# Attention's row maxima, transposed and sent in two halves by query

## The chip, the cores and the metric

The kernel runs on one core of one Trainium2 chip. The metric is device time in microseconds of one execution, lower is better. Engines are named as in the profile: PE (TensorE matmul) with PEld (its weight loads), DVE (VectorE), ACT (ScalarE), POOL (GpSimd), SP (SyncE, whose queue issues nearly all DMAs).

## The reference, cut to what matters

Two transformer layers over 1024 tokens of width 1024, in fp32. Layer 0 mixes with forgetting attention ("fox", 12 heads of 64), layer 1 with latent attention ("mla", 12 heads of 96 with rotary parts). Each layer has 4 more heads that attend to 256 memory tokens, then an output projection and a convolutional feed-forward part. The part around the change is the softmax:

```python
def causal_block_attention(q, k, v, log_decay=None):
    ...
        logits = jnp.einsum('bhqd,bhkd->bhqk', qc, k).astype(jnp.float32)
        if log_decay is not None:
            logits = logits + args[2][..., None] - log_decay[:, :, None, :]
        ...
        logits = jnp.where(key_idx[None, :] <= q_idx[:, None], logits, -jnp.inf)
        p = jax.nn.softmax(logits, axis=-1).astype(v.dtype)
        return jnp.einsum('bhqk,bhkd->bhqd', p, v)

def memory_cross(qm, k_mem, v_mem, q_gain, k_gain):
    ...
    logits = jnp.einsum('bshd,bmhd->bhsm', q, k).astype(jnp.float32)
    p = jax.nn.softmax(logits, axis=-1).astype(v_mem.dtype)
    return jnp.einsum('bhsm,bmhd->bshd', p, v_mem).reshape(b, s, MEM_WIDTH)
```

## The kernel before, in words

Scores are computed transposed, with keys on the partitions and queries along the free axis, so that the exponentials can be multiplied with V at once. A query's maximum must then be known before its scores are computed: it enters the score product as one more row. `QA` holds a head's queries (64 or 96 rows, plus rows for the decay), and its row `h.mrow` (66 or 96) holds minus the maximum of each of the 1024 queries; `KA` holds ones in that row. A causal head's score products read `QA[0:67]` or `QA[0:97]`. Operands are split into a high and a low part for accuracy; the passes with `KB` or `QB` add the low parts and don't read the row of maxima.

`maxpass(h)` (lines 290 to 315) finds the maxima. It computes a head's scores once with queries on the partitions, in chunks: 10 for a causal head (`CAUSAL_MAX`, lines 59 to 70; the first three cover query tiles 0 to 3, the others tiles 4 to 7), 4 for a memory head (`FULL_MAX`, line 71, two query tiles each). A chunk takes a PSUM buffer `psX` (one of 3, shared with the transposes of queries and keys and with projections), and DVE reduces it: `tensor_reduce` without a mask (L299) or `tensor_tensor_reduce` with the causal mask (L304). The maxima land in `mA`, 128 x 8. `final` (lines 308 to 313) transposes `mA` on PE into a `psX` (8 x 128), DVE negates it into `mrow` (L312), and SP sends it in one DMA into the row of `QA` (L313).

The main loop (lines 428 to 471) goes over 16 heads. A head is cut into units: six groups of two key tiles in a causal head (`CAUSAL_GROUPS`), two in a memory head (`FULL_GROUPS`), and for each group one unit that adds low-part products of an earlier group (`lo`), two units of scores, two of products with V (`hi`): 30 and 10 units in all. Groups 0 and 1 of a causal head are queries 0 to 511, groups 2 to 5 queries 512 to 1023; a memory head's group 0 and group 1 are the two halves. So a head's first scores are its unit 2, and those of the second half begin at unit 12 (causal) or 7 (memory).

Between the units stand the side pieces of later heads: the next head's maxima chunks and `final`, preparation (`prep`: transposes and splits of K and Q) of the next head (`leads` 1) or the one after (`leads` 2), and background work (`bg`: layer 1's group projections). A piece has a position between 0 and 1, and it is run when the count of units done exceeds the position times the units of the head (line 458). Positions stand in `TIMES` (lines 279 to 284), one entry per layer: `max2` and `final2` for causal heads with `leads` 2, `max1`, `final1` with `leads` 1, `max_mem` and `final_mem` while a memory head runs.

Layer 0 runs 12 fox heads, then 4 memory heads, all with `leads` 2. Layer 1 runs 4 memory heads, then 12 mla heads, the first five heads with `leads` 2, the others 1. In layer 1 PE's instructions are kept in program order (`pin[0] = not offset`, line 409); in layer 0 a scheduler orders all engines by priority and by its own model of when operands are ready. Every engine and the SP queue run their instructions in the order in which they stand. `norm1` and `norm2` (lines 392 to 406) divide by the sums on DVE (L404) and send rows over SP (L395 to L399).

```python
add(chunks, *times["max2" if h.causal else "max_mem"])
side.append((times["final2" if h.causal else "final_mem"], final))
...
while side and side[0][0] * total < done:
    side.pop(0)[1]()
```

Of the kernel before, what the change touches and what calls it, by code (L numbers as in the profile page):

```python
# [12 lines left out]
OP = mybir.AluOpType  # L13
# [61 lines left out]
def hybrid_kernel(ctx: ExitStack, tc: tile.TileContext, A, out):  # L75
# [197 lines left out]
    def slot(name="slot", dt=F32):  # L273
# [3 lines left out]


    TIMES = [
        {"prep2": ((0.15, 0.97), (0.25, 0.97)), "max2": (0.0, 0.68), "final2": 0.68, "max_mem": (0.24, 0.75),  # L280
         "final_mem": 0.7, "norm": (7, 24, 27)},
        {"prep1": (0.0, 0.23), "max1": (0.28, 0.76), "final1": 0.8, "prep2": ((0.55, 1.0), (0.38, 1.0)),
         "max2": (0.0, 0.72), "final2": 0.63, "max_mem": (0.0, 0.63), "final_mem": 0.82, "norm": (7, 20, 23)},
    ]

    def attention(L, heads, leads, offset=0, bg=None, fill={}):
# [3 lines left out]
        def maxpass(h):  # L290
            mA = small.tile([P, 8], F32, name="mA")

            def chunk(segs):
                px = psX()
                for qt, k0, nk, off, own, on in segs:
                    mm(px[:, off:off + nk], h.max_q(qt), h.max_k(k0, nk), True, True)
                if not segs[0][4]:
                    q0, n, width = segs[0][0], len(segs), segs[0][2]
                    nc.vector.tensor_reduce(mA[:, q0:q0 + n],  # L299
                                            px[:, :n * width].rearrange("p (a b) -> p a b", a=n), axis=AX, op=OP.max)  # L300
                    return
                for qt, k0, nk, off, own, on in segs:
                    m = mA[:, qt:qt + 1]
                    nc.vector.tensor_tensor_reduce(px[:, off:off + nk], px[:, off:off + nk], mQ[:, 512 - nk:],  # L304
                                                   scale=1.0, scalar=m if on else NEG, op0=OP.add, op1=OP.max,
                                                   accum_out=m)

            def final():
                px = psX()
                transpose(px[:8, :P], mA[:, 0:8], ident)  # L310
                row = small.tile([8, P], F32R, name="mrow")
                nc.vector.tensor_scalar(row, px[:8, :P], -1.0, None, op0=OP.mult)  # L312
                nc.sync.dma_start(h.QA[h.mrow:h.mrow + 1, :].bitcast(F32), row.bitcast(F32))  # L313

            return [lambda c=c: chunk(c) for c in h.max_chunks] + [final]

        def score_units(h, g):
            half, parts = h.groups[g]
# [91 lines left out]
        n = len(heads)  # L410
        later, pend, los = [], [], []
        with tc.high_priority(offset=offset):
            pieces = heads[0].prep() + maxpass(heads[0]) + (heads[1].prep() if leads[1] == 2 else [])
            for i, f in enumerate(pieces):
                f()
                for u in fill.get(i, ()):
                    u()
# [7 lines left out]
                    a[1]()  # L425

        pl.mark = []
        for i, h in enumerate(heads):
            pl.mark.append(tc.cur_priority)
            side = []  # L430

            def add(pieces, a, b):
                side.extend((a + (b - a) * j / len(pieces), f) for j, f in enumerate(pieces))

            if i + 1 < n:
                if leads[i + 1] == 2:
                    *chunks, final = rest if i else maxpass(heads[1])
                    add(chunks, *times["max2" if h.causal else "max_mem"])
                    side.append((times["final2" if h.causal else "final_mem"], final))
                else:  # L440
                    add(heads[i + 1].prep(), *times["prep1"])
                    *chunks, final = maxpass(heads[i + 1])
                    add(chunks, *times["max1"])
                    side.append((times["final1"], final))
            if i + 2 < n and leads[i + 2] == 2:
                add(heads[i + 2].prep(), *times["prep2"][heads[i + 2].row % 2])
                rest = maxpass(heads[i + 2])
# [1333 lines left out]
```

## Time and profile before

| | us |
|---|---|
| median of 3 runs | 2527.43 (2526.28 to 2527.52) |
| the profiled execution, its own time | 2524.9 |
| its span, first to last instruction | 2523.2 |
| PE busy | 2366.4 |
| DVE busy | 1890.5 |
| ACT busy | 1209.2 |
| POOL busy | 980.0 |

The profile is one execution. Busy is the time in which an engine runs at least one instruction; PE's matmuls are pipelined, their ends are modelled, and starts are what can be compared. A wait is idle time of an engine before an instruction, put down to what ended it. PEclk is the granted clock of PE as a share of 2.4 GHz; it is either 1.0 or 0.5 at a time, and a mean over a stretch says how much of it ran at which.

### The profile page before, as it was taken

Reading aid. Unit: us, or ns where it says so; the run is one execution under the profiler, and the core shown is the slowest. Engines: PE = TensorE matmul, PEld = TensorE weight load, DVE = VectorE, ACT = ScalarE, POOL = GpSimd, SP = SyncE. Lnnn points to the kernel's source line nnn. Section 1 sums busy time; section 2 is a strip of 40 time slices with the busy share of each in tenths; the row PEclk is TensorE's granted clock in tenths of the full one; section 3 lists DMA queues with packets and bytes.
Section 4 is the critical chain, followed back from the end, with each engine's and each line's share of the span. In section 5 each row is a group of like instructions: output and inputs, shape, how many; then the busy total and the mean of one; then the engine's idle time right before and its main releaser. Section 6 shows DMA issues by size and latency. Waiting matters only on the chain.

```text
span 2523.2 us, 32480 instructions
## 1 busy us (share of the span) xinstructions
PE 2366.4 (94%) x11609; PEld 1952.9 (77%) x11609; DVE 1890.5 (75%) x3183; ACT 1209.2 (48%) x2341; POOL 980.0 (39%) x640
## 2 busy tenths in 40 slices
PE   7999899998999999989998798879979999998999
PEld 7999666677788888868888676657868888886887
DVE  7432787747778878799997878774488788778997
ACT  5544677723444444434454555555244444443443
POOL 1221467743233233234322566666142333233342
PEclk9999899999999999999999799989999999998999
DMA  4221122252132232541230101010512222225221
GB/s 143 84 51 27 35 61 48 52 182 104 51 92 76 84 92 76 196 154 50 102 134 10 35 22 29 19 38 17 193 60 84 90 77 84 84 84 233 92 101 67
DMA packets 163651, 208.89 MB, mean 83 GB/s; under 512 B 11175, under 2 KB 124682, under 8 KB 163490
## 3 DMA queue, kind: packets, MB, share of 16 engines
q1 hardware_dynamic: 162054, 206.63, 25.8%
q8 instruction: 92, 1.51, 0.2%
q14 instruction: 69, 0.57, 0.1%
q10 hardware_dynamic: 1436, 0.18, 0.0%
HBM read 153.34 MB, written 39.98 MB: 77 GB/s over the span
## 4 chain that ended last, share of the span: by engine, by line
PE 74%; DVE 18%; issue 3%; DMA 3%; ACT 2%; POOL 1%; SPq 0%; DVEq 0%; ACTq 0%; POOLq 0%
PE psX L102 32%; PE psS L102 24%; PE psO L102 15%; DVE f_op L90 2%; PE psX L106 2%; DVE f_x L1156 1%; DVE mA L299 1%; DVE psX L304 1%; DVE f_S L90 1%; POOL f_op L90 1%; DVE KB L525 1%; DVE QB L525 1%; DVE f_d L90 1%; PE psS L106 1%; DVE f_T L90 1%
## 5 line engine op out<-in xcount | busy, mean ns | idle before, releaser
L90 POOL TENSOR_TENSOR f_op<-f_S,f_op 128x512 fp32r<-128x512 f32 x184 | 271.0, 1475 | 670.0 <-ACT f_op L83 613.1
L102 PE MATMUL psS<-f_T,f_op 128*128 128x512 f32 x1584 | 382.2, 393 | 7.8 <-DVE f_T L90 5.9
L90 POOL TENSOR_TENSOR plo<-pf,ph 128x1024 fp32r<-128x1024 f32 (+2 forms) x160 | 312.7, 1966 | 155.0 <-ACT pf L343 96.0
L102 PEld LDWEIGHTS psS<-f_T,f_op 128*128 128x128 f32 x1584 | 297.1, 189 | 68.9 <-DVE f_T L90 6.5
L102 PE MATMUL psX<-f_B,f_op 128*128 128x512 f32 x1260 | 296.3, 389 | 0.1
L83 ACT CAST f_op<-f_S 128x512 fp32r<-128x512 f32 x248 | 153.6, 621 | 269.6 <-PE psS L102 103.2
L102 PEld LDWEIGHTS psX<-f_B,f_op 128*128 128x128 f32 x1260 | 236.4, 188 | 49.6 <-issue 0.5
L102 PE MATMUL psS<-f_op 128*128 128x512 f32 x960 | 222.4, 390 | 1.6 <-DVE f_op L90 1.5
L102 PEld LDWEIGHTS psS<-f_op 128*128 128x128 f32 x960 | 180.6, 188 | 40.1 <-DVE f_op L90 2.4
L102 PE MATMUL psX<-f_op 128*128 128x512 f32 x666 | 174.5, 403 | 19.9 <-DVE f_op L90 16.5
L102 PE MATMUL psX<-w_w,hTh 128*128 128x384 f32 (+2 forms) x672 | 168.1, 334 | 2.2 <-ACT hTh L83 2.2
L102 PEld LDWEIGHTS psX<-f_op 128*128 128x128 f32 x666 | 128.1, 194 | 52.4 <-DVE f_op L90 21.7
L83 ACT CAST f_op<-f_raw 128x512 fp32r<-128x512 f32 x148 | 91.4, 622 | 136.2 <-PE psS L102 70.4
L342 ACT ACTIVATE ph<-psS 128x1024 fp32r<-128x1024 f32 (+2 forms) x131 | 112.3, 858 | 87.7 <-PE psS L102 79.1
L898 DVE SCALAR_TENSOR_TENSOR f_v<-f_cv,cw,f_v 128x1023 f32<-128x1023 f32 x88 | 150.2, 1706 | 5.0 <-ACT f_v L896 3.5
L102 PE MATMUL psX<-KA,QA 66*128 66x128 f32 (+4 forms) x320 | 110.3, 392 | 28.9 <-DVE mA L299 11.3
L83 ACT CAST f_op<-f_d 128x512 fp32r<-128x512 f32 x144 | 84.3, 619 | 102.0 <-PE psS L102 35.6
L858 DVE TENSOR_TENSOR f_u<-psS,f_p 128x512 f32<-128x512 f32 x44 | 30.4, 691 | 126.6 <-PE psS L102 126.6
L102 PEld LDWEIGHTS psX<-w_w,hTh 128*128 128x128 f32 x672 | 120.9, 190 | 3.2 <-ACT hTh L83 2.8
L898 DVE SCALAR_TENSOR_TENSOR f_v<-f_cg,cw,f_v 128x1023 f32<-128x1023 f32 x88 | 112.7, 1280 | 11.0 <-ACT f_v L896 11.0
L90 POOL TENSOR_TENSOR f_op<-f_d,f_op 128x512 fp32r<-128x512 f32 x52 | 74.1, 1425 | 116.9 <-ACT f_op L83 112.8
L102 PE MATMUL psS<-QA,KA 67*128 67x512 f32 (+7 forms) x304 | 110.0, 363 | 8.3 <-DMA QA<-mrow 8.3
(379 smaller groups left out, 5693.2 us busy)
## 6 DMA issues: line engine op xcount, KB each, us to landing
f_raw<-in_ffn_w_up_dram SPq DMA_DIRECT2D x88, 512.0 KB
g<-f_v SPq DMA_DIRECT2D x44, 512.0 KB
f_d<-g SPq DMA_DIRECT2D x36, 512.0 KB
f_d<-in_ffn_w_down_dram SPq DMA_DIRECT2D x36, 512.0 KB
w_raw<-in_fox_w_in_dram SPq DMA_DIRECT2D x48, 192.0 KB
rrow<-rec SPq DMA_DIRECT2D x32, 256.0 KB
wo_raw<-in_w_out_dram SPq DMA_DIRECT2D x32, 256.0 KB
xr<-x SPq DMA_DIRECT2D x16, 512.0 KB
```

The lines of the kernel that those rows point to most:

```text
L83: nc.scalar.copy(o, i)
L90: return (nc.vector if eng == "v" else nc.gpsimd).tensor_tensor(o, a, b, op=OP.subtract)
L102: r = nc.tensor.matmul(*a, **k)
L106: r = nc.tensor.transpose(*a, **k)
L299: nc.vector.tensor_reduce(mA[:, q0:q0 + n], px[:, :n * width].rearrange("p (a b) -> p a b", a=n), axis=AX, op=OP.max)
L304: nc.vector.tensor_tensor_reduce(px[:, off:off + nk], px[:, off:off + nk], mQ[:, 512 - nk:], scale=1.0, scalar=m if on else NEG, op0=OP.ad ...
L342: nc.scalar.activation(ph, ps[:, :w], AF.Exp)
L525: nc.vector.scalar_tensor_tensor(Tl[tl0:tl1, hs], px, gcol, Th[0:n, hs].bitcast(F32), op0=OP.mult, op1=OP.subtract)
L858: nc.vector.tensor_tensor(o, x, y, op=OP.add)
L898: nc.vector.scalar_tensor_tensor(v[:, k:], src[:, :S - k], cw[:, 2 - k, ch:ch + 1], v[:, k:], op0=OP.mult, op1=OP.add)
L1156: nc.vector.tensor_tensor(X[t][:, hs], X[t][:, hs], self.sets[st][v], op=OP.add)
```

## The change

The transposition of `mA` is cut in two, by query halves. `final(half)` transposes 4 columns, negates 4 x 128 and sends 512 values into its half of the row. The first half is placed one and a half chunk intervals behind the chunk after which all its maxima are known (`first`, 3 for causal heads, 2 for memory heads), so behind the chunk with index 4 of 10 or 3 of 4. The second half is carried over into the head itself, to position 0.08: after unit 3 of a causal head and after unit 1 of a memory head. The chunks' stretches in `TIMES` end later (0.68 to 0.85 in layer 0's `max2`, 0.76 to 0.92 in layer 1's `max1`, and so on); the `final` positions go. The first head of a layer runs both halves one after the other, where it ran `final` before.

```diff
     TIMES = [
-        {"prep2": ((0.15, 0.97), (0.25, 0.97)), "max2": (0.0, 0.68), "final2": 0.68, "max_mem": (0.24, 0.75),
-         "final_mem": 0.7, "norm": (7, 24, 27)},
-        {"prep1": (0.0, 0.23), "max1": (0.28, 0.76), "final1": 0.8, "prep2": ((0.55, 1.0), (0.38, 1.0)),
-         "max2": (0.0, 0.72), "final2": 0.63, "max_mem": (0.0, 0.63), "final_mem": 0.82, "norm": (7, 20, 23)},
+        {"prep2": ((0.15, 0.97), (0.25, 0.97)), "max2": (0.0, 0.85), "max_mem": (0.24, 0.85), "norm": (7, 24, 27)},
+        {"prep1": (0.0, 0.23), "max1": (0.28, 0.92), "prep2": ((0.55, 1.0), (0.38, 1.0)),
+         "max2": (0.0, 0.85), "max_mem": (0.0, 0.8), "norm": (7, 20, 23)},
     ]
...
-            def final():
+            def final(half):
                 px = psX()
-                transpose(px[:8, :P], mA[:, 0:8], ident)
-                row = small.tile([8, P], F32R, name="mrow")
-                nc.vector.tensor_scalar(row, px[:8, :P], -1.0, None, op0=OP.mult)
-                nc.sync.dma_start(h.QA[h.mrow:h.mrow + 1, :].bitcast(F32), row.bitcast(F32))
-
-            return [lambda c=c: chunk(c) for c in h.max_chunks] + [final]
+                transpose(px[:4, :P], mA[:, half * 4:half * 4 + 4], ident)
+                row = small.tile([4, P], F32R, name="mrow")
+                nc.vector.tensor_scalar(row, px[:4, :P], -1.0, None, op0=OP.mult)
+                nc.sync.dma_start(h.QA[h.mrow:h.mrow + 1, half * 512:half * 512 + 512].bitcast(F32), row.bitcast(F32))
+
+            first = max(j for j, segs in enumerate(h.max_chunks) if segs[0][0] < 4) + 1
+            return [lambda c=c: chunk(c) for c in h.max_chunks], first, [lambda i=i: final(i) for i in range(2)]
...
+            chunks, first, ends = maxpass(heads[0])
+            pieces = heads[0].prep() + chunks + [lambda: [f() for f in ends]] + (heads[1].prep() if leads[1] == 2 else [])
...
+        carried = []
         for i, h in enumerate(heads):
-            side = []
+            side, carried = carried, []
...
-                    *chunks, final = rest if i else maxpass(heads[1])
-                    add(chunks, *times["max2" if h.causal else "max_mem"])
-                    side.append((times["final2" if h.causal else "final_mem"], final))
+                    chunks, first, ends = rest if i else maxpass(heads[1])
+                    span = times["max2" if h.causal else "max_mem"]
                 else:
                     add(heads[i + 1].prep(), *times["prep1"])
-                    *chunks, final = maxpass(heads[i + 1])
-                    add(chunks, *times["max1"])
-                    side.append((times["final1"], final))
+                    chunks, first, ends = maxpass(heads[i + 1])
+                    span = times["max1"]
+                add(chunks, *span)
+                side.append((span[0] + (span[1] - span[0]) * (first + 1.5) / len(chunks), ends[0]))
+                carried.append((0.08, ends[1]))
```

## Rows read from the trace of the kernel before

**Rows 1.** The page: engine, busy us, share of the span, instructions.

```profile
PE 2366.4 (94%) x11609; PEld 1952.9 (77%) x11609; DVE 1890.5 (75%) x3183; ACT 1209.2 (48%) x2341; POOL 980.0 (39%) x640
```

**Rows 2.** Waits of PE, 277 to 515 us: us in total, times, longest.

```profile
PE psX L106 <- DVE mA L304: 9.2, 9, 2.2
PE psS L102 <- DMA QA<-mrow: 3.6, 2, 2.2
PE psX L102 <- DVE mrow L312: 2.7, 1, 2.7
```

**Rows 3.** Waits of PE, 1360 to 1765 us.

```profile
PE psX L102 <- DVE mA L299: 11.3, 8, 5.0
...
PE psX L106 <- POOL gk L93: 7.9, 4, 4.2
PE psX L106 <- DVE mA L304: 7.7, 4, 2.7
PE psS L102 <- DMA QA<-mrow: 4.7, 3, 3.3
PE psX L106 <- DVE mrow L312: 3.0, 1, 3.0
```

**Rows 4.** Windows: length, busy us (count) of PE, PEld, DVE, ACT, POOL; PEclk, DMA share, GB/s.

```profile
291.00:475.00 184.00, 169.44 (x939) 123.11 (x938) 148.60 (x309) 143.88 (x214) 128.75 (x69) 0.95 0.22 51
...
1450.00:1740.00 290.00, 253.15 (x1508) 196.33 (x1508) 216.83 (x454) 163.37 (x251) 187.25 (x118) 0.95 0.10 27
```

**Rows 5.** PE groups: count | busy, mean ns | idle before; whole span, then 283:520.

```profile
L106 PE MATMUL psX<-ident,mA 128*8 128x128 f32 x32 | 9.5, 297 | 13.9 <-DVE mA L304 11.5 <-DVE rs_y L233 1.4 <-DVE mA L299 1.1
...
L106 PE MATMUL psX<-ident,mA 128*8 128x128 f32 x15 | 4.2, 282 | 3.8 <-DVE mA L304 3.8
```

**Rows 6.** PE in order of time, layer 1: start, us, instruction [idle before].

```profile
1574.95 0.27 PE L106 MATMUL psX<-ident,mA 128*8 128x128 f32 x1 [1.68 <-DVE mA L304]
...
1579.19 0.64 PE L106 MATMUL psX<-ident,gk 128*96 128x128 f32 x4 [1.26 <-POOL gk L93]
...
1600.42 0.39 PE L102 MATMUL psO<-ph,g_vh 128*65 128x512 f32 x1
1600.65 0.40 PE L102 MATMUL psO<-ph,g_vl 128*64 128x512 f32 x1
1600.97 0.27 PE L106 MATMUL psX<-ident,mA 128*8 128x128 f32 x1
1601.00 0.45 PE L102 MATMUL psX<-g_w,LTh 128*128 128x192 f32 x2
```

**Rows 7.** DVE in order of time, the same boundary of two heads in layer 1.

```profile
1574.09 0.75 DVE L304 CUSTOM_DVE_ANT_0 psX<-psX,mQ,mA 128x512 f32<-128x512 f32 x1
...
1577.57 0.27 DVE L312 TENSOR_SCALAR mrow<-psX 8x128 fp32r<-8x128 f32 x1
...
1577.97 1.71 DVE L93 TENSOR_TENSOR gk<-gk,rs_y 128x512 f32<-128x512 f32 x2
```

**Rows 8.** SP's issues of the row, and the scores that waited for it.

```profile
473.81 0.69 SPq L313 DMA_DIRECT2D QA<-mrow  x1
...
477.68 0.50 PE L102 MATMUL psS<-QA,KA 67*128 67x512 f32 x1 [1.40 <-DMA QA<-mrow]
...
1473.58 0.70 SPq L313 DMA_DIRECT2D QA<-mrow  x1
...
1475.43 0.79 PE L102 MATMUL psS<-QA,KA 97*128 97x512 f32 x1 [3.33 <-DMA QA<-mrow]
```

**Rows 9.** PE, layer 0: last score of group 0 with the row, first of group 2, two heads.

```profile
342.97 0.34 PE L102 MATMUL psS<-QA,KA 67*128 67x384 f32 x1
...
345.69 0.40 PE L102 MATMUL psS<-QA,KA 67*128 67x512 f32 x1
...
426.04 0.34 PE L102 MATMUL psS<-QA,KA 67*128 67x384 f32 x1
...
430.64 0.40 PE L102 MATMUL psS<-QA,KA 67*128 67x512 f32 x1
```

More of the change, by code (lines that the diff above doesn't have):

```diff
@@ L412, in attention @@
         with tc.high_priority(offset=offset):
-            pieces = heads[0].prep() + maxpass(heads[0]) + (heads[1].prep() if leads[1] == 2 else [])
+            chunks, first, ends = maxpass(heads[0])
+            pieces = heads[0].prep() + chunks + [lambda: [f() for f in ends]] + (heads[1].prep() if leads[1] == 2 else [])
             for i, f in enumerate(pieces):
```

## The prediction

> **What bounds the kernel now.** I read the page's engine shares first, then TensorE's waits in the two attention stages, then windows, then the time lines around the places that the change moves. TensorE is busy 94% of the span and VectorE 75% [rows 1], so the time goes where TensorE's idle time goes. The change touches only attention: about 283 to 520 us (layer 0) and 1370 to 1760 us (layer 1). Its possible gain is what TensorE loses there, not a share of the whole.
>
> What it loses is written in two tables. In layer 0 it waited 9.2 us at transposes until VectorE had finished masked maxima (L304), 3.6 us in front of scores until the row of maxima had landed, 2.7 us for a PSUM buffer that the row's negation (L312) still held [rows 2]. In layer 1: 11.3 us for unmasked maxima (L299), 7.7 for masked ones, 4.7 for the row; and 7.9 for keys that GpSimd scales, which this change doesn't touch [rows 3]. The windows add the clock: in 184 us of layer 0 and in 290 us of layer 1 the mean grant was 0.95 of full speed [rows 4]. The two levels are 2.4 and 1.2 GHz, so a tenth of these stretches, 18 and 29 us, ran at 1.2 GHz; at the higher level that work takes half as long, so 9 + 14.5 = 23.5 us are lost in this way.
>
> **The change, part by part.** Its positions are counted in units of a head (30 in a causal head, 10 in a memory head). Layer 0, causal: the last maxima moves from unit 19 to 23, the transpose of the first half from 21 to 12; the second half's goes to unit 3 of the head itself. Layer 1, causal: last maxima 22 to 26, first half 25 to 18, second half again unit 3. A head's first scores are its unit 2, those that need the second half its unit 12 (memory heads: transposed at 1, needed at 7).
>
> *1. The transpose no longer stands behind its own maxima.* All transposes of maxima waited 13.9 us, 1.4 of it (for rs_y) in the first head, which the change leaves as it is; layer 0's share is 3.8 [rows 5], so layer 1's is 8.7. The first half now follows its last maxima by two and a half intervals, the second by 7 to 10 units. Layer 0's 3.8 us and 3.7 us around layer 1's memory heads go whole. The other 5.0 us are three waits of 1.68 us, one of them in the rows, each followed 4 us later by a wait for scaled keys of about 1.3 us [rows 6]: TensorE arriving earlier would wait longer there, unless VectorE, which gets to the keys only after the maxima and the negation [rows 7], is earlier too. I count half, 2.5. Together -10.0, with bounds -7.5 and -12.5.
>
> *2. The first scores no longer wait for the row.* 8.3 us in both layers [rows 2, 3]. The first half leaves 7 to 9 units earlier between causal heads. Between memory heads of layer 0 it leaves at unit 8 of 10 as now, so the 2.2 us there stays. I take -5.0, bounds -3 and -6.1.
>
> *3. Maxima spread wider.* Their interval grows from 2.04 to 2.55 units in layer 0 and from 1.44 to 1.92 in layer 1. They share three psX buffers with transposes and projections; the waits that this can shorten are layer 1's 11.3 us for L299 maxima, 5.4 us of layer 0's 9.2, and the 2.7 and 3.0 for L312 [rows 2, 3, 5], some 22 us. But nothing in VectorE's work shrinks, and maxima now run into the stretch in which the next head's operands are split. I take a little under a quarter, -5.0; bounds +5 (they collide there) and -12.
>
> *4. Clock.* 23.5 us are lost to the lower level [rows 4]; idle time in these windows is 14.6 + 36.9 = 51 us, of which parts 1 to 3 take 20, or two fifths. Proportionally that gives back 9; spells at 1.2 GHz also follow waits that stay, so I take -4.0; bounds 0 and -9.
>
> *5. One more transpose for each of 32 heads.* Around one that waited for nothing, TensorE started 0.32 us after a 512-column matmul that itself had started 0.23 after the one before, and the next instruction came 0.03 later [rows 6]: about 0.09 + 0.03 = 0.12 us more than without it. A half has four columns where a whole has eight; the trace has no such transpose, so between 0 and the 0.30 us mean of a record [rows 5] I take 0.1: +3.2 (0 to +9.5).
>
> *6. The second half's row must come in time.* The trace of before has no such wait. The way from the transpose is 0.27 us, as long for the negation [rows 6, 7], 0.1 between them and to the issue, and then the landing: a whole row issued at 1473.58 let the scores go at 1475.43, 1.85 us later, and one at 473.81 only at 477.68, 3.87 us later [rows 8]. **Does half a row land sooner?** The trace has only whole rows, and I price the half like the whole, 1.85, with 0.9 as the low end (in proportion to bytes) and 3.9 as the high. The Trainium skill (DMA: Bandwidth & Descriptors, section Anatomy of one DMA) says the setup and completion part, about 2.0 us for the path it fits, depends on nothing of the transfer, which speaks against splitting: by it two halves cost two landings and part 6 stays at +6, by proportion it would be near 0. No run here shows it yet. So 2.5 us are needed plus VectorE's queue, which is in order: the negation can stand behind other work, 2.35 us of it in the case of [rows 6, 7]. The cover is 8 units. In layer 0, score to score, it was 2.72 us in one head and 4.60 in another [rows 9]; in layer 1, where 290 us hold some eleven heads [rows 4], eight of 30 units are 7 us. So layer 0's 11 causal heads are exposed by about 0.3 us on average (0 to 1.5), and seven memory heads, with 5 units, by 0.4: +6 (0 to +21).
>
> *7. VectorE, SP and POOL.* 32 more negations of 0.27 us [rows 7] are 9 us on an engine that is busy 81% of one window and 75% of the other [rows 4]; a quarter shows: +2 (0 to +9). SP issues 32 more transfers of about 0.7 us [rows 8]; behind a late row on that queue stand the copies QA to QB and KA to KB of the head after next, needed most of a head later, so I count 0. POOL gets nothing.
>
> **Sum.** -10.0 - 5.0 - 5.0 - 4.0 + 3.2 + 6 + 2 = -12.8 us. Against the profiled execution's own 2524.9 us: 2512.1. The median of the runs stands 2.5 us above that execution, so I predict 2514.6 us.
>
> **Rivals.** *A. The waits only move.* Keys that GpSimd scales (7.9 us, [rows 3]) and VectorE's queue set the end of layer 1's pairs, and layer 0's gain is eaten by part 6. For it: the two waits of [rows 6], one behind the other. Against it: VectorE has a quarter of its time free. Then parts 1 to 4 give only 11 against 11 of cost: 2527, within 2523 to 2532. 18%.
>
> *B. A bigger gain.* The late row is what holds each second head of layer 0, and without it waits and clock come back at the bounds: -12.5 - 6.1 - 8 - 7 against 7 of cost (part 6 at 2) make -27 us, 2500. 18%.
>
> *C. Slower: the second half's row is late in each head.* In layer 0 the negation stands behind VectorE's products with the reciprocals or psX maxima, and TensorE stops at unit 12. At 1.5 us for 11 heads and 1.0 for 7, part 6 is 23.5; 4 us of clock given back turn into 4 lost, so the sum is -20 + 5.2 + 23.5 + 4 = +12.7: 2540. It decides from a mean of about 1.0 us over the 18 heads, where the gains of parts 1 to 4 (24, less 5.2 of other cost) are used up. Against it: layer 0's instructions aren't pinned to program order (line 409), and other matmuls can fill. 10%.
>
> *D. The split isn't one.* If the second write to the row held up all readers of that buffer, the scores of units 7 and 8 would wait for it, some 1.5 us in 27 causal and memory heads with the clock behind it: some 2550 (the forecast without part 6, and 40 us). 4%.
>
> **How the numbers follow.** The forecast has 50%, from 2506 to 2522. About 5 us, 0.2%, is what a measurement of this kernel can tell from no change. Faster by more: forecast and B, 0.68; within: A, 0.18; slower: C and D, 0.14. The range 2498 to 2534 reaches over A, most of B and a third of C; left out are B's far end, most of C, and D, some 16%.
>
> **What would show it.** Right: transposes of maxima wait under 2 us in all outside the first head; scores' waits for the row under 5 us; grants in both windows 0.96 or more; 64 transposes and 64 negations. Wrong: a score of 67 or 97 rows in a head's third group with a wait of over 1 us for the row in most heads (C), in the second group (D); waits for scaled keys grown by what the transposes lost (A). I would be wrong altogether if TensorE's idle time in both stages stayed while the waits changed names.

## The result and the profile after

The changed kernel takes 2544.24 us (median of 4 runs, 2539.81 to 2544.85), the kernel before 2526.86 us beside it: a ratio of 1.0076, 95% interval 1.0060 to 1.0091. It is **slower** by 15 to 23 us, 0.8%; 2514.6 us had been forecast, and the measurement lies beyond the range. The profiled execution after took 2543.93 us with a span of 2542.2.

Page of the changed kernel, engine shares, to set beside [rows 1]:

```profile
PE 2376.0 (93%) x11641; PEld 1960.3 (77%) x11641; DVE 1905.8 (75%) x3215; ACT 1210.3 (48%) x2341; POOL 976.7 (38%) x640
```

TensorE and VectorE each have the 32 instructions more that the change adds, and busy times 9.6 and 15.3 us longer. TensorE's waits in layer 0 (277 to 525 us: us in total, times, longest), to set beside [rows 2]; the wait in the last line is the only one of its kind in the whole span:

```profile
PE psO L102 <- DVE oh L85: 7.2, 2, 5.8
PE psX L102 <- DVE mA L303: 4.0, 2, 2.5
...
PE psX L106 <- DVE mA L303: 2.6, 2, 1.7
...
PE psS L102 <- DMA QA<-mrow: 0.2, 1, 0.2
```

The same view of layer 1 (1360 to 1765 us), beside [rows 3]; L298 and L303 are the unmasked and masked maxima that were L299 and L304:

```profile
PE psX L102 <- DVE mA L298: 20.8, 13, 5.5
PE psX L106 <- DVE gq L93: 8.5, 4, 2.7
PE psX L106 <- DVE mA L303: 7.5, 4, 3.6
PE psX L106 <- DVE mA L298: 7.0, 2, 4.4
...
PE psX L106 <- DVE gk L93: 2.9, 3, 1.0
```

What the change was to remove is gone: scores waited 8.3 us for a row before [rows 2, 3] and 0.2 us in the whole span after. What it was to relieve grew. Layer 1's wait for unmasked maxima in front of chunks and projections, 11.3 us in [rows 3], is 20.8 us, with 7.0 at transposes (2.2 before), and the wait for keys that GpSimd scales (7.9 us, with 0.9 for queries on VectorE) is replaced by 8.5 + 2.9 us for queries and keys that VectorE scales. Transposes of maxima, which should no longer wait, waited as long as in [rows 5]. Their group in the changed kernel (count, min/median/max ns, first and last start; then idle time by what ended it):

```profile
L106 PE MATMUL psX<-ident,mA x64: 269/273/421, 281.1 to 1755.8; 128*4 128x128 f32 x64
...
  DVE mA L303: 8.5, 5
  DVE mA L298: 3.5, 2
```

With 2.0 us for three other operands that is 14.0 us against 13.9, though not at the same places: the three waits of 1.7 us in layer 1's pairs of heads are gone, and waits of 2.61 us (at 1438.86), 3.65 (1477.54), 1.56 (1719.74) and 0.74 stand at other boundaries. The windows, beside [rows 4], show that the clock went the other way too:

```profile
291.00:475.00 184.00, 166.71 (x909) 119.20 (x908) 150.53 (x307) 137.79 (x205) 123.72 (x67) 0.94 0.21 48
1450.00:1740.00 290.00, 248.05 (x1458) 194.56 (x1457) 221.72 (x465) 162.03 (x247) 175.80 (x118) 0.92 0.10 28
```

A mean grant of 0.92 between the levels 2.4 and 1.2 GHz is 16% of 290 us, 46 us, at 1.2 GHz where it was 29; half of the additional 17 us is lost time. TensorE gets through 1458 matmuls in a window that held 1508, though the windows hold work a few us apart, since layer 1 starts 8.5 us later.

Over the whole of each stage, layer 0 and layer 1, the kernel before and then the changed one (length, busy us of PE to POOL, PEclk, DMA share, GB/s):

```profile
282.20:620.00 337.80, 311.76 (x1575) 233.03 (x1575) 241.76 (x487) 201.93 (x299) 193.44 (x105) 0.95 0.30 83
1386.90:1762.50 375.60, 325.84 (x1863) 252.53 (x1862) 271.12 (x555) 206.84 (x316) 231.85 (x147) 0.92 0.10 26
```

```profile
281.10:628.00 346.90, 315.81 (x1591) 233.74 (x1591) 251.78 (x502) 200.19 (x296) 192.99 (x104) 0.94 0.28 80
1395.40:1781.00 385.60, 330.14 (x1872) 258.60 (x1871) 277.23 (x571) 208.08 (x316) 224.92 (x147) 0.90 0.10 26
```

Layer 0 is 9.1 us longer and layer 1 10.0. TensorE's idle time, length less busy, grew by 5.1 and 5.7 us; the rest is busy time, 4.1 and 4.3 us more, for a few more transposes and at lower grants.

**Where in layer 1.** One boundary of two heads, the pattern of [rows 6, 7]. TensorE, then VectorE, in order of time:

```profile
1593.70 0.61 PE L106 MATMUL psX<-ident,gk 128*96 128x128 f32 x4 [0.96 <-DVE gk L93]
...
1597.78 1.09 PE L106 MATMUL psX<-ident,gq 128*96 128x128 f32 x4 [2.68 <-DVE gq L93]
```

```profile
1592.21 0.75 DVE L303 CUSTOM_DVE_ANT_0 psX<-psX,mQ,mA 128x512 f32<-128x512 f32 x1
...
1592.88 3.18 DVE L93 TENSOR_TENSOR gk<-gk,rs_y 128x512 f32<-128x512 f32 x2
1595.98 2.61 DVE L93 TENSOR_TENSOR gq<-gq,rs_y 128x768 f32<-128x768 f32 x2
```

In the kernel before, behind the gk of [rows 7]:

```profile
1579.61 3.04 DVE L93 TENSOR_TENSOR gq<-gq,rs_y 128x768 f32<-128x768 f32 x2
```

The late maxima stand ahead of the next head's keys and queries in VectorE's queue. TensorE takes its instructions in program order here, so the transposes of gk and gq hold it, and behind them the scores. The two scalings of gk took 3.18 us where [rows 7] had 1.71; those of gq took 2.61 where they had 3.04. From one transpose of maxima to the one a pair of heads later (1559.46 to 1614.24 here, 1574.95 to 1628.35 before) TensorE waits 7.2 us in place of 6.0, and the pair takes 54.8 us in place of 53.4. The pairs are not all of layer 1's loss: from its first transpose of maxima to the fifth head's row of sums (issued at 1487.43 before, 1500.61 after) it takes 4.7 of its 10 us more, and there waits for unmasked maxima of 4.39, 3.09 and 2.61 us stand between the memory heads.

**Where in layer 0.** The boundary whose scores [rows 9] show at 342.97 and 345.69. TensorE, then VectorE:

```profile
341.74 0.50 PE L102 MATMUL psX<-KA,QA 66*128 66x128 f32 x2 [1.52 <-DVE mA L303]
343.21 0.27 PE L106 MATMUL psX<-ident,mA 128*4 128x128 f32 x1 [0.97 <-DVE vh L1382]
...
347.12 0.40 PE L102 MATMUL psS<-QA,KA 67*128 67x512 f32 x1
```

```profile
338.57 2.48 DVE L530 SCALAR_TENSOR_TENSOR KB<-k,g_cols,KA 64x512 fp32r<-64x512 f32 x1
...
342.27 0.74 DVE L303 CUSTOM_DVE_ANT_0 psX<-psX,mQ,mA 128x512 f32<-128x512 f32 x1
```

L530 splits operands of the head after next. The last maximum ends at 343.01, behind such splits, and the second half's transpose starts at 343.21. Its first score starts at 347.12, 1.43 us later than in the kernel before, but no wait stands in front of that one: TensorE had other work. At the end of the layer a single wait of 5.81 us stands before the products with V: the copy of their PSUM buffer stood in VectorE's queue behind two products that took 5.64 us. VectorE there, and GpSimd:

```profile
517.59 5.64 DVE L93 TENSOR_TENSOR oh<-oh,rrow 128x512 f32<-128x512 f32 x2 [1.20 <-DMA rrow<-rec]
523.15 0.68 DVE L85 COPY oh<-psO 65x512 f32<-65x512 f32 x1
```

```profile
517.58 5.10 POOL L90 TENSOR_TENSOR plo<-pf,ph 128x1024 fp32r<-128x1024 f32 x2 [3.15 <-ACT pf L344]
```

### The profile page after: what moved, and what is told of

Same layout as the page of the kernel before. It is cut to its first block, busy times and chain, and to the rows that moved or that the text cites. A ratio compares the mean times of both kernels' runs of the same rounds, so it can differ in the third digit from the quotient of the medians.

```text
span 2542.2 us, 32676 instructions
## 1 busy us (share of the span) xinstructions
PE 2376.0 (93%) x11641; PEld 1960.3 (77%) x11641; DVE 1905.8 (75%) x3215; ACT 1210.3 (48%) x2341; POOL 976.7 (38%) x640
## 4 chain that ended last, share of the span: by engine, by line
PE 55%; DVE 15%; issue 3%; ACT 1%; POOL 1%; DMA 1%; SPq 0%; DVEq 0%; ACTq 0%; POOLq 0%
PE psX L102 23%; PE psS L102 21%; PE psO L102 9%; DVE f_op L90 2%; PE psX L106 1%; DVE f_x L1161 1%; POOL f_op L90 1%; DVE mA L298 1%; DVE psX L303 1%; DVE f_S L90 1%; DVE f_T L90 1%; DVE rs_y L233 1%; DVE gq L90 1%; DVE f_d L90 1%; DVE g_ss L1556 1%
## 5 line engine op out<-in xcount | busy, mean ns | idle before, releaser
L102 PEld LDWEIGHTS psX<-f_B,f_op 128*128 128x128 f32 x1260 | 236.4, 188 | 49.6 <-issue 0.5
L344 ACT ACTIVATE pf<-psS 128x1024 f32<-128x1024 f32 (+2 forms) x131 | 111.9, 854 | 4.4 <-POOL plo L90 4.4
```

The source lines that it names most:

```text
L102: r = nc.tensor.matmul(*a, **k)
L344: nc.scalar.activation(pf, ps[:, :w], AF.Exp)
```

## The experiments

Eighteen kernels ran; the medians of the kernel before beside them were 2524.09 to 2524.87 us. For each the table gives the median, the ratio to the kernel before on the same chip with its interval, and the lengths of the two attention stages in its one profiled execution: layer 0 from its first transpose of maxima to the first matmul of the feed-forward part (before: 282.2 to 620.0 us), layer 1 from its first transpose of maxima to its last product with g_vh (1386.9 to 1762.5).

| kernel | median us | ratio, 95% | layer 0 | layer 1 |
|---|---|---|---|---|
| before | 2526.86 | 1 | 337.8 | 375.6 |
| after | 2544.24 | 1.0076 (1.0060–1.0091) | 346.9 | 385.6 |
| e1 split, old stretches | 2527.42 | 1.0006 (0.9993–1.0020) | 350.4 | 371.1 |
| e2 whole row, wide | 2557.69 | 1.0133 (1.0105–1.0162) | 341.4 | 399.0 |
| e3 split, old stretches and places | 2535.75 | 1.0047 (1.0032–1.0062) | 353.8 | 372.2 |
| e4 second row step | 2548.58 | 1.0094 (1.0060–1.0127) | 359.5 | 380.4 |
| e5 after, negation on ScalarE | 2541.07 | 1.0065 (1.0045–1.0085) | 344.9 | 387.4 |
| e6 split in layer 1 only, old stretches | 2521.38 | 0.9988 (0.9977–1.0000) | 336.3 | 376.8 |
| e7 row finished at 0.72 | 2523.15 | 0.9993 (0.9982–1.0005) | 335.8 | 377.4 |
| e8 maxima in 0.66 | 2521.69 | 0.9993 (0.9983–1.0004) | 337.4 | 375.7 |
| e9 split, wide in layer 0 only | 2535.57 | 1.0037 (1.0021–1.0053) | 345.7 | 371.8 |
| e10 layer 1 split and wide, layer 0 old | 2535.73 | 1.0036 (1.0020–1.0053) | 335.5 | 388.9 |
| e11 transposes twice | 2533.82 | 1.0034 (1.0014–1.0054) | 333.9 | 379.1 |
| e12 transfers twice | 2522.88 | 0.9990 (0.9973–1.0006) | 334.1 | 376.2 |
| e13 split, layer 0 tighter | 2534.39 | 1.0038 (1.0024–1.0053) | 354.4 | 367.5 |
| e14 e6, layer 1 tighter | 2536.69 | 1.0044 (1.0028–1.0061) | 335.5 | 388.1 |
| e15 e6, second half at 0.15 | 2521.20 | 0.9988 (0.9978–0.9999) | 342.7 | 371.3 |
| e16 e6, layer 0 whole and tighter | 2538.79 | 1.0052 (1.0039–1.0065) | 355.6 | 373.5 |
| e17 negations twice | 2531.84 | 1.0041 (1.0024–1.0058) | 340.5 | 375.3 |
| e18 second row step, layer 0 only | 2549.05 | 1.0096 (1.0078–1.0114) | 350.7 | 372.4 |

A stage of one execution is good to some 6 us only: e6 and e15 have the same layer 0, and their stages differ by 6.4. The profiled execution can also lie far from the median of its kernel (e18 12.2 us below, e4 9.0 and e15 8.1 above). In layer 1 the wide versions stand clear all the same: whole row with old stretches 372.4 to 379.1 (380.4 with e4's second step), split with old stretches 367.5 to 376.8, split and wide 385.6 to 388.9.

Medians of different sets of runs are subtracted below. By the ratios, each taken against the kernel before beside it, the differences come out up to 2.3 us smaller or 2.0 larger, and each is good to some 4 to 6 us only.

### e1 to e4: the stretches or the split

The changed kernel with the old stretches (**e1**), the kernel before with the wide ones (**e2**):

```diff
 # e1, against after (layer 0; layer 1 likewise 0.76, 0.72, 0.63)
-"max2": (0.0, 0.85), "max_mem": (0.24, 0.85)
+"max2": (0.0, 0.68), "max_mem": (0.24, 0.75)
 # e2, against before (layer 0; layer 1 likewise, final1 0.94, final2 0.87, final_mem 0.82)
-"max2": (0.0, 0.68), "final2": 0.68, "max_mem": (0.24, 0.75), "final_mem": 0.7
+"max2": (0.0, 0.85), "final2": 0.87, "max_mem": (0.24, 0.85), "final_mem": 0.87
```

> The changed kernel with the old stretches of the maxima (they end at 0.68 and 0.76 again); both halves stay, the second one still carried into the head. Theory 1, late maxima: the second half cannot leave before the last maxima are done, and the wider stretches put these 4 units later, into VectorE's fullest time; so the loss goes and the time is 2512 to 2530 us. Theory 2, price of the split: 32 more transposes, negations, row transfers and PSUM buffers cost the 17 us, wherever the maxima stand; then 2538 to 2548. Theory 3, order by chance: layer 0's order comes from a scheduler and any edit moves it by some 10 us; then layer 0 (start of the first feed-forward part) lies anywhere within 620 to 632 us without following either theory.

> The kernel before with the wider stretches of the change and the whole row sent as before, a little behind the last maxima (0.87 and 0.87 in layer 0, 0.94 and 0.82 in layer 1). Theory 1, late maxima: the loss comes with the stretches, and here even the first scores wait for the last maxima: 2540 to 2565 us. Theory 2, price of the split: there is no split here, so within 2522 to 2534 us.

Without the wide stretches the loss is gone (2527.42), and with them alone it is larger than the change's (2557.69). So the stretches carry it, mostly in layer 1: 399.0 us where the whole row is late as well, 385.6 in the changed kernel, 371.1 in e1. The two losses are not the same one, though: in e2's layer 1 TensorE waits 40.9 us at transposes of maxima for masked maxima, 7.2 to 8.2 us in every second head, and the changed kernel has no wait of that kind over 3.7 us.

**e3** puts the second half where the whole row had been sent, in place of carrying it into the next head; **e4** gives the kernel before a second row step in each head, to a spare place that nothing reads:

```diff
 # e3, against e1
-carried.append((0.08, ends[1]))
+side.append((last, ends[1]))
 # e4, against before, at the end of final()
+px = psX()
+transpose(px[:8, :P], mA[:, 0:8], ident)
+row = small.tile([8, P], F32R, name="mrow")
+nc.vector.tensor_scalar(row, px[:8, :P], -1.0, None, op0=OP.mult)
+nc.sync.dma_start(spare_d.rearrange("(j p) -> j p", p=P), row.bitcast(F32))
```

> The changed kernel with the old stretches, and the second half not carried: it stands where the whole row stood before (0.68, 0.7, 0.8, 0.82), only the first half leaves earlier. Theory 1, late maxima: no loss, 2515 to 2530 us. Theory 2, price of the split: 2538 to 2548 us, since all instructions of the split are there. If the first run is fast and this one near 2527, the carrying is what gains.

> The kernel before, and behind each transpose of maxima a second one with its own PSUM buffer, negation and row transfer (to a spare place in DRAM that nobody reads): the bare price of 32 more such steps. Theory 1 and my prediction's parts 5 and 7: 3 to 7 us more than before, 2530 to 2534 us. Theory 2, price of the split: 12 us more or above, 2539 to 2548 us.

Carrying the second half is worth 8 us (2535.75 against 2527.42). And an extra row step that nobody waits for costs 24 us: there is a price of the step, which e11, e12, e17 and e18 take apart below.

### e5, e7, e8: the held bank, and order by chance

```diff
 # e5, against after
-nc.vector.tensor_scalar(row, px[:4, :P], -1.0, None, op0=OP.mult)
+nc.scalar.activation(row, px[:4, :P], AF.Identity, scale=-1.0)
 # e7 and e8, against before, layer 0
-"max2": (0.0, 0.68), "final2": 0.68
+"max2": (0.0, 0.68), "final2": 0.72      # e7
+"max2": (0.0, 0.66), "final2": 0.68      # e8
```

> The changed kernel with one instruction of each half moved: the negation of the transposed maxima is done by ScalarE, not VectorE. Theory A, the held bank: in layer 0 what costs is that each transposed half holds one of the three psX buffers until VectorE, which still has maxima and evictions ahead of the negation, comes to it (held 53.4 us in 32 pieces there in the changed kernel, 16.8 us in 16 before). Then layer 0's attention falls from 346.9 us to about 340, psX is held under 30 us there, the half-clock time falls from 42.0 towards 36, and the run is about 2536. Theory B, order by chance: layer 0's order was only drawn anew, no single wait carries it; then the attention of layer 0 moves by up to 6 us in either direction without regard to how long psX is held. Theory C, the spread maxima themselves are late: the negation is not what is late, so both layers stay within 3 us of 346.9 and 385.6, run 2541 to 2548.

> The kernel before with one number moved that does nothing of its own: in layer 0 the row of maxima is finished at 0.72 of the head in place of 0.68. Theories A and C: no step added, no stretch widened, so layer 0's attention stays within 3 us of 337.8 and the ratio is 0.999 to 1.001. Theory B (the order alone moves layer 0 by 10 us): layer 0's attention comes out 5 to 15 us off, ratio 1.002 to 1.006 or below 0.998.

> The kernel before with layer 0's maxima in 0.66 of a head in place of 0.68, a second edit that hardly does anything of its own. Theories A and C: layer 0's attention within 3 us of 337.8, ratio 0.999 to 1.001. Theory B: 5 to 15 us off in either direction, ratio beyond 1.002 or below 0.998.

With the negation on ScalarE the run is 2541.07: some 3 us may be won, within the intervals, not the 8 expected. But the test didn't do what it was to do: psX was held for 46.3 us in layer 0 (transpose's start to negation's end, summed) where 53.4 had been, so little was freed. The held bank is neither shown nor excluded. The two small shifts changed nothing (0.9993 each), so neither place is critical to 0.02 or 0.04 of a head. They reorder little, though (287 and 13 of TensorE's 11609 instructions stand at another place in its order), so they don't exclude that layer 0's scheduler, which draws the order anew when instructions are added, found a worse one.

### e6, e9, e10: layer by layer

**e6** keeps layer 0 as before and splits layer 1 with the old stretches; **e10** is e6 with layer 1's wide ones; **e9** is the changed kernel with layer 1's old ones:

```diff
 # e6, against e1
-return [lambda c=c: chunk(c) for c in h.max_chunks], first, [lambda i=i: final(i) for i in range(2)]
+ends = [lambda i=i: final(4 * i, 4) for i in range(2)] if L else [lambda: final(0, 8)]
 # e9, against after; e10 the other way round, against e6 (layer 1)
-"max1": (0.28, 0.92), "max2": (0.0, 0.85), "max_mem": (0.0, 0.8)
+"max1": (0.28, 0.76), "max2": (0.0, 0.72), "max_mem": (0.0, 0.63)
```

> Layer 0 as before the change (whole row, old stretches); layer 1 split and carried, but with the old stretches. If the two layers add, as theories A and C both say, layer 0's attention is 337 to 340 us as before and layer 1's 371 us as in the run of the split with old stretches: 2526.9 - 4.5 = about 2521, ratio 0.998. If the gain of layer 1 in that run was chance of one profile (theory B), layer 1's attention comes out between 371 and 380 and the ratio between 0.998 and 1.002.

> The changed kernel, split in both layers, with layer 1's maxima back in their old stretches and layer 0's left wide. Theory of the late maxima (the wide stretches put layer 1's last maxima beside the next head's evictions of gq and gk, and TensorE waits for psX): layer 1's attention falls from 385.6 us to 371 to 377, TensorE's waits for maxima there fall from 33.7 us to under 20, layer 0 stays at 345 to 350, and the run is 2544 - 11 = about 2533. If it is layer 0's wide stretches that cost, the run stays at 2540 to 2546.

> Layer 0 as before the change; layer 1 as the changed kernel has it, split, carried and wide. Theory of the late maxima: layer 1's attention is 383 to 389 us with waits for maxima over 30 us, layer 0's 336 to 338, and the run is 2521.4 (the split in layer 1 alone) + 12 = about 2533. If the two layers don't add, because layer 1 only looked slow for want of a good state left by layer 0, it is under 2526.

TensorE's waits in layer 1, e6 and then e10, 1360 to 1765 us:

```profile
PE psX L102 <- DVE mA L298: 8.4, 8, 2.2
PE psX L106 <- POOL gk L93: 8.3, 3, 3.0
...
PE psX L106 <- DVE mA L298: 5.6, 3, 3.5
PE psX L106 <- DVE mA L303: 3.3, 3, 1.3
...
PE psX L102 <- DVE mA L303: 2.2, 1, 2.2
...
PE psX L106 <- DVE gk L93: 2.0, 1, 2.0
...
PE psX L106 <- DVE gq L93: 1.7, 3, 0.8
```

```profile
PE psX L102 <- DVE mA L298: 20.4, 13, 5.5
PE psX L106 <- DVE gq L93: 8.6, 4, 2.7
PE psX L106 <- DVE mA L303: 7.7, 4, 3.6
PE psX L106 <- DVE mA L298: 7.2, 2, 4.6
...
PE psX L106 <- DVE gk L93: 3.0, 3, 1.0
```

This is layer 1's loss, alone: waits for maxima of 19.5 us become 35.3, and the median goes from 2521.38 to 2535.73, 14.4 us. The waits for gq and gk change their place and not their sum: 11.6 us, all on VectorE, where e6 has 8.3 on GpSimd and 3.7 on VectorE. By the same subtraction layer 0's wide stretches cost 8.2 us (e9 less e1), and layer 0's split 6.0 (e1 less e6). The profile of e9 doesn't place its 8.2 us: its layer 0 is no longer than e1's, and between its two attention stages lie 769.9 us against 762.9, a length that varies from 762.5 to 770.5 among these profiles without any edit there. The split in layer 1 alone may gain: e6 (with e15) is the fastest version here, with the ratio 0.9988 and an interval that just reaches 1; e15, which differs from it in one position, has the same ratio in twelve runs of its own (0.9978 to 0.9999). But e7 and e8, which change next to nothing, have 0.9993, and e12, which only adds work, 0.9990. So a gain of 3 us is about the least that can be told here, and it isn't told apart from those.

### e13 to e16: the other direction

If late maxima cost, earlier ones should gain.

```diff
 # e13, against e1, layer 0
-"max2": (0.0, 0.68), "max_mem": (0.24, 0.75)
+"max2": (0.0, 0.60), "max_mem": (0.24, 0.66)
 # e16, against e6, layer 0
-"max2": (0.0, 0.68), "final2": 0.68, "max_mem": (0.24, 0.75), "final_mem": 0.7
+"max2": (0.0, 0.60), "final2": 0.60, "max_mem": (0.24, 0.66), "final_mem": 0.62
 # e14, against e6, layer 1
-"max1": (0.28, 0.76), "max2": (0.0, 0.72), "max_mem": (0.0, 0.63)
+"max1": (0.28, 0.70), "max2": (0.0, 0.65), "max_mem": (0.0, 0.56)
 # e15, against e6
-carried.append((0.08, ends[1]))
+carried.append((0.15, ends[1]))
```

> The split with old stretches in both layers (2527.4), layer 0's maxima now tighter: 0.60 of a head, 0.24 to 0.66 before a head over the memory. If layer 0 pays for the split because its maxima end late at the boundary of a head, this gives back most of its 6 us: 2520 to 2523, ratio 0.997 to 0.999. If each extra row step has its price wherever it stands, nothing comes back: 2526 to 2530, ratio 1.000 to 1.002.

> Split in layer 1 alone (2521.4), its maxima now tighter than before the change (0.70, 0.65 and 0.56 in place of 0.76, 0.72 and 0.63). If TensorE's waits grow with the place of the last maximum, going earlier by half the step of the change wins up to half of the 14 us it cost, waits for maxima in layer 1 fall under 17 us and the run is 2514 to 2520. If the old stretches were already at the flat end, or VectorE's queue is now crowded earlier in the head, 2520 to 2528.

> Split in layer 1 alone with old stretches, the second half sent at 0.15 of the head that uses it in place of 0.08. If the second half's row has slack there, as the vanished waits for the row say, nothing changes or 1 to 2 us of waits for its maxima go: 2519 to 2522. If its slack is under 0.07 of a head (about 2 us), its scores wait for the row as in the kernel before: 2524 to 2532.

> Split in layer 1 alone, layer 0's whole row made from maxima in 0.60 and 0.24 to 0.66 of a head, sent at 0.60 and 0.62. If layer 0's stretches were at the flat end, layer 0's attention stays within 3 us of 336 and the run is 2519 to 2524. If late maxima cost layer 0 even before the change, it falls to 330 to 333 and the run to 2515 to 2519. If crowding is what costs, it rises by over 4 us.

Three of the four went against the theory of late maxima: tighter stretches cost 7.0 us (e13 less e1), 15.3 (e14 less e6) and 17.4 (e16 less e6). TensorE's waits in layer 1 of e14:

```profile
PE psX L102 <- DVE mA L298: 13.6, 15, 4.0
PE psX L106 <- DVE gq L93: 10.9, 4, 2.8
```

The waits for maxima are not the ones that grew: 19.7 us in the whole view, 19.5 in e6. Nor are those for gk and gq together, 12.0 us in both. But in e6 8.3 of these are for GpSimd's part, and here 10.9 are for gq, which stands behind slower scalings of gk on VectorE. At one boundary two of them took 5.37 us, beside three subtractions on GpSimd (plo, the low parts of the exponentials), where [rows 7] have 1.71:

```profile
1522.02 5.37 DVE L93 TENSOR_TENSOR gk<-gk,rs_y 128x512 f32<-128x512 f32 x2
```

```profile
1521.51 6.73 POOL L90 TENSOR_TENSOR plo<-pf,ph 128x1024 fp32r<-128x1024 f32 x3
```

Layer 1 is 11.3 us longer than in e6. TensorE's idle time there grew from 44.7 to 49.6 us, in small waits, and its busy time from 332.1 to 338.5 us for the same work (1875 and 1873 matmuls), at mean grants of 0.91 and 0.90. In e10 it was idle time alone that grew, to 56.2 us, with 332.8 busy.

So the theory has to be put differently: the old stretches lie between two worse places, and up to a tenth of a head earlier, or 0.10 to 0.17 later, costs more than the split can win. That a place of the maxima matters by what it makes coincide on VectorE and GpSimd is a reading of these rows; no run tries it alone. e15 says that the second half's row has slack in layer 1: 0.07 of a head later, nothing changes.

Part of these losses is clock. Each run comes with its mean granted clock. It was 0.9638 of full speed on average in e16 and 0.9688 in the kernel before beside it. A mean of 0.9638 is 7.2% of the time at 1.2 GHz, and if half of that time is lost, as the prediction counts it, the difference makes some 13 of e16's 15 us over the kernel before. By the same estimate it is some 16 of e18's 24 us (0.9628), 5 of e10's 11 (0.9666) and 9 to 10 of the changed kernel's 17 to 19 (0.9653). The waits alone therefore don't price a place.

### e11, e12, e17, e18: what a row step costs

```diff
 # each against before, in final()
 # e11
+transpose(px[:8, :P], mA[:, 0:8], ident)
 # e12
+nc.sync.dma_start(spare_d.rearrange("(j p) -> j p", p=P), row.bitcast(F32))
 # e17
+nc.vector.tensor_scalar(small.tile([8, P], F32R, name="mrow"), px[:8, :P], -1.0, None, op0=OP.mult)
 # e18: e4 with this ahead of the second step
+if L:
+    return
```

> The kernel before with each row's transpose run twice into the same bank: TensorE's part of an extra row step and nothing else, 32 transposes more. If TensorE's own time is the price of the split, this costs 32 x 0.4 to 0.7 us = 13 to 22 us, ratio 1.005 to 1.009 (as a whole second row step did, 2548.6). If the price is the bank that is held and the place in VectorE's queue, the transposes alone cost 32 x 0.1 = 3 us, ratio 1.000 to 1.002.

> The kernel before with each row sent a second time, to a spare place: the extra transfer of a second row step and nothing else, 32 transfers more in SyncE's queue. If transfers are the price of the split, ratio 1.005 to 1.009. If the price is the bank and VectorE's queue, the queue of SyncE hides them: ratio 0.999 to 1.001.

> The kernel before with each row's negation done twice on VectorE from the same bank: 32 operations of 0.27 us more, nothing else. If the price of a row step is VectorE's queue, this costs 32 x 0.27 = 9 us or more, ratio 1.0035 to 1.006. If it is the second bank (or the transposes), VectorE's free quarter hides them: ratio 0.999 to 1.0015.

> The second row step (bank, transpose, negation, transfer to a spare place) in layer 0's 16 heads alone. If layer 0 pays the most of the 24 us that both layers cost, as one execution of each had it (22 of layer 0, 5 of layer 1): 2524 + 16 to 22, ratio 1.006 to 1.009. If each of 32 steps costs the same: 2536, ratio 1.004 to 1.0055. If the 24 us came mostly from the order of layer 1: ratio under 1.003.

Transfers are free (e12, -2.5 us, interval -6.8 to +1.5). The transpose costs 8.6 us for 32 (3.5 to 13.6) and the negation 10.3 (6 to 15), where the prediction's estimate for the transposes was 3.2 us and the negations' own durations are 8.7 us, of which most had been thought hidden. The sum of the three is 16 us, the whole second step 24 (15 to 32): the second bank may add the rest, but the intervals overlap. And as far as the intervals tell, all of it is layer 0's: 16 steps there cost 24.2 us (20 to 29), as much as 32 in both layers, 1.5 us each. The largest of its waits, 277 to 525 us (L305 are its masked maxima), in an execution of 2536.88 us, which shows half of that cost:

```profile
PE psX L106 <- DVE mA L305: 6.7, 6, 2.5
```

No one wait is the price, and for the second negation TensorE waited 1.6 us once. In e17 the largest wait of the same stretch is another:

```profile
PE psO L102 <- DVE oh L85: 6.4, 2, 5.8
```

Its 5.8 us is the changed kernel's wait for a copy behind the two products, for which the kernel before has 0.7 us. That two different edits meet it suggests that it comes with the order in which these operations happen to stand. Whether it is the added instructions' own time in a queue without a gap, or the new order that layer 0's scheduler makes around them, these runs can't tell, since every addition does both.

## Why the prediction was wrong

**Part 3, the wider maxima, is the step that failed.** It was put at -5.0 with +5 as its worst: waits for maxima were to shrink because chunks come less often. The text named what happened ("maxima now run into the stretch in which the next head's operands are split") and priced it from no row. Measured: +14.4 us in layer 1 (e10 less e6; 8.7 by after less e9) and +8.2 in layer 0 (e9 less e1). The reasoning took a wait for L299 as a sign that maxima are too dense. It is a sign of where VectorE is in its queue, and e10 and e14 show that making maxima sparser or denser lengthens it or its neighbours. What [rows 6, 7] already showed, that VectorE reaches gk and gq only after the maxima, was used in part 1 to halve a gain; it should have been used in part 3 to price a loss.

**Part 1, -10.0 for transposes:** nothing of it came in total, 14.0 us of waits against 13.9. The three waits in layer 1's pairs, of which half was counted, went whole; the others came back elsewhere. The half row does follow its last maxima by a distance in program positions. But the distance on VectorE is not that: in layer 0 the maximum stood behind splits until 343.01 while TensorE was already there. In layer 1 the wait of 3.65 us at 1477.54 is one for the half's own last maximum, which started at 1476.73, behind scalings of gk and gq that took 1.87 and 3.99 us.

**Part 2, -5.0 for the row:** right in kind and short in size, 8.3 us became 0.2. It may also be what layer 1 gains from the split: in e6, where no stretch was moved, its waits of 4.7 us for the row are gone and the time is 3.0 us less (0 to 6).

**Part 4, -4.0 for the clock:** followed parts 1 and 3 and so has the wrong sign; from the windows 46 - 29 = 17 us more at 1.2 GHz in layer 1 and about 4 in layer 0, half of it lost, +10.5. The mean grant of the runs says 9 to 10.

**Part 5, +3.2 for transposes (0 to +9.5):** the term was probably too small, +8.6 (3.5 to 13.6) in e11, within its bounds.

**Part 6, +6 for the second half's row:** its wait never came, as the 0.2 us and e15's 0.07 of a head of slack show. Whether half a row lands sooner, which the prediction asked, the one wait for such a row shows:

```profile
454.13 0.64 SPq L312 DMA_DIRECT2D QA<-mrow  x1
```

```profile
455.87 0.51 PE L102 MATMUL psS<-QA,KA 67*128 67x512 f32 x1 [0.22 <-DMA QA<-mrow]
```

That is 1.74 us from issue to score, where the quicker whole row of [rows 8] took 1.85 (e1 has half rows of 1.71 and 1.82), so pricing the half like the whole was right. By what the Trainium skill states for transfers that GpSimd issues (DMA: Bandwidth & Descriptors, section Anatomy of one DMA), setup and completion cost the same whatever the size; this row, issued by SP, agrees. The issue on SP is hardly shorter either, 0.619 us in the median where a whole row's was 0.682, and e12 shows that the number of such transfers costs nothing that can be told.

**Part 7, +2 for the queues (0 to +9):** +10.3 (6 to 15) for the negations alone in e17. "A quarter shows" came from VectorE's mean share of 75 to 81%; at the boundaries of heads, where the negations stand, VectorE can be busy without a break (from 338.57 to 343.40 at the boundary shown above).

Step by step from the kernel before to the changed one, the runs share the loss out: -3.0 (split, layer 1), +6.0 (split, layer 0), +8.2 (wide, layer 0), +8.7 (wide, layer 1, beside the others) make +19.9. Each step starts where the last one ended, so that the sum comes near the measured +19.2 is no test of the shares, and each share is good to some 3 to 6 us. What in layer 0 makes its 14 us of these, single waits, the clock or the scheduler's new order, stays open. Of the rivals, C (2540) was nearest in time, but its mechanism, a late second half in each head, is not what happened; A was right that waits would change their names, but counted that as gains lost and not as a cost.

## What to carry to other kernels

A piece of work that is moved on an in-order engine is priced by what it is moved beside: list the instructions of that engine in the new place and who waits for each, and treat the old place as a point that may be lost in both directions (here 0.10 to 0.17 of a head later cost 8 and 14 us, and 0.06 to 0.09 of a head earlier 7 to 17). A small instruction in a stretch where its engine has no gap can cost about its own time (10.3 us, 6 to 15, for 8.7 us of negations), whatever the mean share of the engine says. When a change bundles a gain with a retuning, split them first: the split row alone, in layer 1, would have lost nothing and perhaps won 3 us.

## What the hardware showed beside this

VectorE's operations with two inputs in SBUF can take several times as long while GpSimd works. The product oh<-oh,rrow, two of 128x512, took 5.64 us at 517.59 beside GpSimd's plo from 517.58 on, where its group's median is 0.69 us for one. A split KB<-k took 2.48 us at 338.57, with GpSimd at otl from 338.11 to 340.50. Its sister that reads one input from PSUM stayed between 730 and 748 ns (minimum, median and maximum ns, changed kernel):

```profile
L93 DVE TENSOR_TENSOR oh<-oh,rrow x32: 675/688/2889, 333.5 to 1794.3; 128x512 f32<-128x512 f32 x32
...
L530 DVE SCALAR_TENSOR_TENSOR KB<-psX,g_cols,KA x36: 730/744/748, 268.2 to 1740.3; 96x512 fp32r<-96x512 f32 x24, 64x512 fp32r<-64x512 f32 x12
L530 DVE SCALAR_TENSOR_TENSOR KB<-k,g_cols,KA x12: 744/822/2962, 269.8 to 452.3; 64x512 fp32r<-64x512 f32 x12
```

The Trainium skill (SBUF — State Buffer, section Who interferes with whom) says that a VectorE instruction with two SBUF inputs meets a GpSimd instruction that reads SBUF at a port they share, and that one with at most one SBUF input doesn't, outside VectorE's two-port modes; these rows agree. It bears on this change. The 12 scalings of gk on VectorE (busy us in total, mean ns), in the kernel before, the changed kernel and e14 (11.8 us in e6):

```profile
L93 DVE TENSOR_TENSOR gk<-gk,rs_y 128x512 f32<-128x512 f32 x12 | 9.5, 827 | 0.1
```

```profile
L93 DVE TENSOR_TENSOR gk<-gk,rs_y 128x512 f32<-128x512 f32 x12 | 16.4, 1401 | 0.0
```

```profile
L93 DVE TENSOR_TENSOR gk<-gk,rs_y 128x512 f32<-128x512 f32 x12 | 23.8, 2019 | 0.0
```

GpSimd works beside them in the kernel before too; what differs is at what. At the boundaries shown it scaled its own part of gk there (2.14 us from 1578.02), and in the changed kernel and in e14 it ran plo (from 1592.97 and 1521.51). How much of layer 1's 14 us (and of e14's 15) is this, and how much the order in the queue alone, was not tried by itself.
